# The low parts of the dense weights: a subtraction on VectorE, or an accumulating DMA

## The chip, the cores and the metric

The kernel runs on one core of a Trainium2 chip. A core has five engines with queues of their own: TensorE (PE in the profile, with PEld for its weight loads), VectorE (DVE), ScalarE (ACT), GpSimd (POOL) and SyncE (SP, which here only issues DMAs). DMAs run on 16 DMA engines of the core. The metric is the device time of one execution in microseconds, as the median of several runs.

## The reference

Two layers of a hybrid diffusion backbone over 512 latent tokens and 256 context tokens, width 1024, everything in float32. What it computes, cut to its products (the kernel's names of the weights):

```
a      = modulate(rms_norm(h))            # 1024 x 768 tokens
proj   = a @ w_in                         # 6656 columns: q, k, v, pool, Hyena inputs, gates
attn   = differential attention(q, k, v) @ w_attn_o
pool   = windowed means, mixed per group  @ w_pool_o
hyena  = two long convolutions, gated     @ w_hy_o
h      = h + g * ((sig0 * attn + sig1 * pool + sig2 * hyena) @ w_out)
h      = h + g * ((silu(gate) * up) @ w_ffn_out),  gate | up = modulate(rms_norm(h)) @ w_ffn_in
```

In layer 0 all 768 tokens go through; in layer 1 the context tokens give keys and values alone, so most of its products have 512 columns.

## The kernel before

Features lie on the 128 partitions, tokens along the free dimension. A float32 product is made of three products of shorter numbers: each operand is split into a high part, with the significand that one pass of TensorE carries, and a low part, the rest; TensorE then accumulates high*high, high*low and low*high in PSUM. The activations are split once. The weights are split as they come in.

The dense products go through `units` (L257). A unit is a list of steps; a step makes one tile of 128 output features (two tiles for the branch projections, which have only 4 input tiles): it loads up to 1024 weights per partition (512 KB) into `raw`, tag "wr" with 3 buffers, from SP's queue (L265); splits them by `split_to` (L250), a cast on ScalarE to `wh` (L252) and a subtraction on VectorE to `wl` (L253), tags "wh" and "wl" with 2 buffers each; and issues 8 x 3 matmuls for each range of token columns (L277), then its eviction. There are 328 steps. In layer 0 a step has two ranges, 512 and 256 columns, so 48 matmuls; in layer 1 one range of 512, so 24. Where a norm has to be finished for one range of tokens before the other (`cuts`: the output projection, the first units of the feed-forward, its last part), steps run over one range alone; those over 256 columns are the short steps.

The other work: the Hyena convolutions are done as block spectra, with transforms on TensorE and complex products on VectorE (`T`, `Y`, L801 to L822); their filters (`fa`, L695) likewise; attention has scores, exponentials and transposes. Modulation vectors are products and sums on VectorE from rows (`mr`) that SP loads beside everything else. Gate values and Hyena outputs go to DRAM and come back (`gsp`, `ysp`).

The order of the work: `PROG` and `HEAD` are orders written out by hand that mix convolution stages, attention and dense steps; within that a planner orders each engine's queue by priority and by when operands and buffers come free. From layer 0's first projections on, the weights' split has a priority 3000 instructions ahead (`ahead`, L957), so that it runs as soon as there is a buffer. Every queue is worked off in order. GpSimd has only 8 memsets: 4 constants and 4 that clear `qz` (L1201) before each layer's attention. Two other places borrow buffers of the tag "wr": three of the modulation weights' loads at the start (L382) and rows of `mod_steps` (L491).

Of the kernel before, what the change touches and what calls it, by code (L numbers as in the profile page):

```python
# [10 lines left out]
F32 = mybir.dt.float32  # L11
# [23 lines left out]
# columns of the vectors that hold one value per feature: first column, count of columns  # L35
# [6 lines left out]
# stages of the convolutions  # L42
# [67 lines left out]
def layouts(inp):  # L110
    """The inputs in the order in which the kernel reads them; every element is copied as it is."""
# [36 lines left out]
def build(ctx: ExitStack, tc: tile.TileContext, io: dict, out: bass.AP, dbg=None):  # L148
# [17 lines left out]
    def half(side, name, **tags):  # L166
        """Buffers on one side of the free memory, in this order, in place of those that the side had:
        tag = (bytes per partition, count)."""
        shut(side)
        st = ExitStack()  # L170
        pool = st.enter_context(tc.tile_pool(name=f"{name}_{side}", bufs=1, reuse_waits="tile", side=side))
        ph[side] = (st, tags)
        for t, (size, cnt) in tags.items():
            assert t not in tg, t
            tg[t] = (pool, size, cnt)
            pool.tile([P, size // 4], F32, tag=t, name=nm("first"), bufs=cnt)
# [25 lines left out]
    def FB(tag, n, dt=F32, shape=None):  # L202
        """Buffers of the background work: "fl" lives long, "fg" over two steps, "fx" shortly."""
        return PT(tag if tag in tg else "b", n, shape or [P, 512], dt)
# [22 lines left out]
    class Acc:  # L227
        """Output of a product for some ranges (first, count) of the 768 token columns."""
# [13 lines left out]
        def segs(self):  # L242
            """Per range."""
            return [(a, c, n) for a, (c, n) in zip(self.aps, self.rng)]

        def pieces(self):
            """As few contiguous pieces as there are."""
            return self.whole

    def split_to(hi, lo, src):  # L250
        """hi + lo = src, each with the significand that one pass carries."""
# [5 lines left out]
    def units(src, K, mts, xs, rng, evict):  # L257
        """A product cut into steps: a step loads and splits 1024 weights per partition or fewer, K of each
        output feature, multiplies and evicts. src(m): the weights of the step from output tile m on."""
        per = 2 if K <= 4 else 1  # L260

        def step(m):
            n = K * per * P
            raw = wp.tile([P, 1024], F32, tag="wr", name=nm("wr"), bufs=3)
            SP.dma_start(out=raw[:, 0:n], in_=src(m))  # L265
            wh = wp.tile([P, 1024], F32R, tag="wh", name=nm("wh"), bufs=2)
            wl = wp.tile([P, 1024], F32R, tag="wl", name=nm("wl"), bufs=2)
            with tc.high_priority(offset=ahead[0]):
                split_to(wh[:, 0:n], wl[:, 0:n], raw[:, 0:n])
# [29 lines left out]
    def spread(r, j0, n):  # L299
        """Columns of per-token values to a row, the same on every partition."""  # L300
# [6 lines left out]
    def sumsq_add(st, hk, c0, n):  # L307
        """st: per range, the sum over feature tiles of squares, one value per partition and token."""
# [15 lines left out]
    def norm_steps(hs, st, rng, g, sh, a):  # L324
        """Normalise and modulate one range of tokens into the split tiles of a, in steps."""
# [19 lines left out]
    def norm_more(n=1):  # L345
        """Emit n steps of the norm that goes on beside the products."""
# [13 lines left out]
    def first_norm(hs, mlp):  # L360
        """The first norm with the two vectors that it needs: the scale on TensorE, the shift on VectorE, as
        their weights arrive. The tokens come token-major and are scaled before they are transposed."""
# [15 lines left out]
        def load_shift():  # L378
            i = len(rows)
            src = io["w_mod"][0][i * P:(i + 1) * P, 0:1024]  # L380
            if i < 7:
                t = PT("y", "wm", [P, 1024]) if i < 4 else wp.tile([P, 1024], F32, tag="wr", name=nm("wr"), bufs=3)  # L382
# [91 lines left out]
    def mod_steps(todo):  # L474
        """Further vectors, one feature per partition, from the rows of the transposed weights: product and sum
        on VectorE, in steps. todo: (layer, vector, rows, streams)."""
# [7 lines left out]
        for l, n, i, nv in todo:  # L484
            pr = SM("pr", 32, bufs=1)
            pv = pr[:].rearrange("p (v h m) -> p v h m", v=2, h=2)
            for m in range(8):
                if "fx" in tg:
                    raw = [FB("fx", "mr")[:] for _ in range(2)]
                else:  # L490
                    t = wp.tile([P, 1024], F32, tag="wr", name=nm("mr"), bufs=3)  # L491
# [21 lines left out]
    def step():  # L513
        """One step of the work that waits in the background: what it weighs, or None."""
# [8 lines left out]
    def pump(n=1):  # L523
        """Emit steps that weigh n together."""
# [6 lines left out]
    def settle():  # L531
        """Go on to a point where the background work holds no buffer of the phase."""
# [3 lines left out]
    def finish(n=0):  # L536
        """Go on until n pieces of work are left."""
# [3 lines left out]
    def norm_cols(l, which, nv):  # L541
        """Columns gain*(1+scale) and shift for the norm before the mixers (0) or before the FFN (1)."""
# [41 lines left out]
    def sin_of(dst, src, b, f):  # L584
        """dst = sin(f * (src + b)), the argument brought into [-pi, pi] first."""
# [10 lines left out]
    def mlp_steps(l, res):  # L596
        """Hidden features of the filters, by lag and by descending lag in each block: the high parts on the half
        of the partitions of that number, the low parts on the other half."""
# [37 lines left out]
    def w3_cols(l, cg):  # L636
        """The last filter layer's weights of 128 channels, both directions and orders, on both halves of the
        partitions: high parts, low parts."""
# [6 lines left out]
    def filter_steps(l, mlp, cg, lat, rinv, seg_out):  # L645
        """Spectra of the kernel segments of 128 channels, both orders, segment 0 being the lowest lag:
        seg_out(segment) is called with a function that writes to a place [P, order, re/im, channel];
        and the inverse of the norm of order 0 and of the product of both norms, a column each."""
# [11 lines left out]
        def seg(dl, cur, cb, pr, pb):  # L660
            """K[dl] from the spectra of the lag blocks dl (cur, at cb) and dl - 1 (pr, at pb)."""
# [10 lines left out]
        for n, p in enumerate(pairs):  # L672
# [26 lines left out]
            if p == 0:  # L699
                # channel norms, a column per order, and the bias as a term of lag 0 on that scale  # L700
# [28 lines left out]
    def spectra(l, mlp, cg, lat):  # L729
        """The same into a tile [P, segment, order, re/im, channel]."""  # L730
# [9 lines left out]
    def spectra_steps():  # L740
        """The spectra of layer 1, in steps, to DRAM: re, im - re, re + im."""
# [19 lines left out]
    def load_spectra(cg):  # L761
        """The spectra of layer 1 of 128 channels, a tile [P, segment, part, channel] per order."""
# [8 lines left out]
    def forward(vh, vl, nb, parts):  # L771
        """Spectra of nb blocks of 128 tokens: [P, (-im, re, im) or (re + im, re, -im), block, channel]."""
# [18 lines left out]
    def spectral(K, oo, U, nb):  # L791
        """Products of the spectra, summed over the input blocks: [P, block, re/im, channel]."""
# [15 lines left out]
    def spectral_parts(K, U):  # L808
        """The same for four blocks with three real products each, from K = re, im - re, re + im."""
# [15 lines left out]
    class Conv:  # L825
        """Both long convolutions of 128 channels of one stream, in stages; the result replaces x2."""
# [67 lines left out]
    def hyena_in(l, a, cg):  # L894
        """The Hyena inputs of 128 channels after their short convolution, v, x1, x2: the units and their results."""
# [21 lines left out]
    swap = list(range(16, 32)) + list(range(0, 16))  # L917

    def layer(l, a, hs, first, prepare):
# [18 lines left out]
        # Hyena input with its short convolution, the long ones, and the gates between them  # L938
# [24 lines left out]
        def stage(what):  # L963
            """The next stage of a kind: gates (g), Hyena inputs (h), and of the convolutions, small letters for
# [573 lines left out]
```

## Time and profile before

| | before |
|---|---|
| time, three runs | 2394.32, 2396.85, 2397.19 us |
| median | 2396.85 us |
| the profiled execution | span 2393.1 us; its own time is not listed, 3.75 us beside the span lead to the median |
| granted TensorE clock, mean | 0.990 |
| busy: TensorE, VectorE, ScalarE, GpSimd | 97%, 73%, 41%, 0% |
| DMA | 302.47 MB, mean 126 GB/s |

A share of busy time is a mean over very different stages: the convolutions of layer 0 (about 60 to 720 us) load VectorE most, the feed-forward of layer 1 (about 2000 to 2393 us) almost only TensorE. The granted clock has two levels, 1.2 and 2.4 GHz; 1.00 in a stretch means 2.4 GHz throughout. A step's name in the rows is `d<-ah,wh` (or `hh`, `gh`, `xs`): product into PSUM tile d from activations and weights.

### The profile page before, as it was taken

The numbers are of one execution on the slowest core, as the hardware profiler recorded it, in microseconds if no ns is written. First come the engines' busy times: TensorE is split into PE (matmuls) and PEld (weight loads), VectorE is DVE, ScalarE is ACT, GpSimd is POOL, SyncE is SP. The second block draws the span as 40 slices with busy tenths as digits, with TensorE's granted clock in tenths as the row PEclk, the third lists the DMA queues.
The fourth block names the chain that finished last, engine by engine and source line by source line (L and its number), as shares of the span: only waits on it lengthen the run. The fifth ranks groups of instructions, "written<-read, shape, count | busy, mean of one in ns | idle before, by whom it ended". The sixth has DMA issues, their size and how long they took to land. (4 is left out here: it accounts for less than half of the span.)

```text
span 2393.1 us, 33367 instructions
## 1 busy us (share of the span) xinstructions
PE 2328.9 (97%) x12830; PEld 1981.6 (83%) x12830; DVE 1737.3 (73%) x3174; ACT 982.2 (41%) x1678; POOL 2.7 (0%) x8
## 2 busy tenths in 40 slices
PE   7999899999989999999999999999999999999998
PEld 2888788888878888888888888888888789888888
DVE  7688878899888785666768736899888778333336
ACT  6434343457772452111133424433377635322223
POOL 0000000000000000000000000000000000000000
PEclk9999899999999999999999999999999999999999
DMA  7132122322137553444725435344311444332224
GB/s 256 65 104 79 50 91 86 115 90 81 36 118 268 181 169 117 130 145 154 235 92 179 153 106 169 121 169 161 119 57 46 168 149 156 115 97 95 92 95 151
DMA packets 117369, 302.47 MB, mean 126 GB/s; under 512 B 13397, under 2 KB 27349, under 8 KB 116186
## 3 DMA queue, kind: packets, MB, share of 16 engines
q1 hardware_dynamic: 117210, 300.34, 37.2%
q8 instruction: 101, 1.65, 0.3%
q14 instruction: 58, 0.48, 0.1%
HBM read 266.74 MB, written 33.55 MB: 125 GB/s over the span
## 5 line engine op out<-in xcount | busy, mean ns | idle before, releaser
L277 PE MATMUL d<-ah,wh 128*128 128x512 f32 (+1 forms) x2336 | 712.1, 354 | 7.7 <-ACT si L1381 2.8
L252 ACT CAST wh<-wr 128x1024 fp32r<-128x1024 f32 (+3 forms) x328 | 331.6, 1011 | 936.2 <-PE d L277 770.2
L277 PE MATMUL d<-al,wh 128*128 128x512 f32 (+1 forms) x2336 | 713.9, 354 | 0.6 <-DVE al L470 0.5
L277 PE MATMUL d<-ah,wl 128*128 128x512 f32 (+1 forms) x2336 | 711.9, 353 | 2.1 <-DVE wl L253 2.0
L253 DVE TENSOR_TENSOR wl<-wr,wh 128x1024 fp32r<-128x1024 f32 (+3 forms) x328 | 384.4, 1173 | 161.3 <-ACT wh L252 150.0
L277 PEld LDWEIGHTS d<-ah,wh 128*128 128x128 f32 x2336 | 390.7, 188 | 72.7 <-ACT wh L252 3.4
L277 PEld LDWEIGHTS d<-ah,wl 128*128 128x128 f32 x2336 | 391.8, 189 | 63.8 <-DVE wl L253 3.0
L277 PEld LDWEIGHTS d<-al,wh 128*128 128x128 f32 x2336 | 392.1, 189 | 62.3 <-DVE al L340 0.8
L498 DVE SCALAR_TENSOR_TENSOR junk<-mr,cb 128x512 bf16<-128x512 f32 x256 | 176.2, 688 | 11.8 <-DMA mr<-in_w_mod_rows_dram 6.5
L277 PE MATMUL d<-hh,wh 128*128 128x512 f32 (+1 forms) x584 | 178.3, 339 | 3.7 <-DVE h L1416 3.7
L277 PE MATMUL d<-hh,wl 128*128 128x512 f32 (+1 forms) x584 | 177.6, 339 | 0.0
L277 PE MATMUL d<-hl,wh 128*128 128x512 f32 (+1 forms) x584 | 177.4, 339 | 0.0
L1390 DVE TENSOR_TENSOR si<-d,si 128x512 f32<-128x512 f32 (+2 forms) x48 | 36.9, 768 | 175.5 <-PE d L277 175.5
L277 PE MATMUL d<-xs,wh 128*128 128x512 f32 x576 | 144.6, 358 | 0.8 <-ACT mx L1193 0.5
L1416 DVE SCALAR_TENSOR_TENSOR h<-d,mod,h 128x512 f32<-128x512 f32 (+1 forms) x96 | 58.3, 614 | 81.3 <-PE d L277 79.7
L277 PEld LDWEIGHTS d<-hh,wh 128*128 128x128 f32 x584 | 102.0, 189 | 17.6 <-issue 4.0
L277 PEld LDWEIGHTS d<-hh,wl 128*128 128x128 f32 x584 | 101.8, 189 | 12.8
L277 PEld LDWEIGHTS d<-hl,wh 128*128 128x128 f32 x584 | 101.8, 189 | 12.8 <-DVE hl L253 0.2
L277 PEld LDWEIGHTS d<-xs,wh 128*128 128x128 f32 x576 | 94.7, 189 | 17.5 <-ACT mx L1193 0.9
L277 PE MATMUL d<-xs,wl 128*128 128x512 f32 (+1 forms) x288 | 87.3, 356 | 0.0
L805 DVE TENSOR_TENSOR Y<-Y,T 128x1024 f32<-128x1024 f32 (+1 forms) x80 | 84.5, 1056 | 0.2
L804 DVE TENSOR_TENSOR T<-U,K 128x1024 f32<-128x1024 f32 (+1 forms) x80 | 83.2, 1057 | 0.0
(296 smaller groups left out, 3211.4 us busy)
## 6 DMA issues: line engine op xcount, KB each, us to landing
wr<-in_w_in_dram SPq DMA_DIRECT2D x104, 512.0 KB, 3.3
wr<-in_w_ffn_in_dram SPq DMA_DIRECT2D x96, 512.0 KB, 3.4
mr<-in_w_mod_rows_dram SPq DMA_DIRECT2D x160, 256.0 KB, 3.3
wr<-in_w_out_dram SPq DMA_DIRECT2D x32, 512.0 KB, 4.2
ksp<-K SPq DMA_DIRECT2D x28, 384.0 KB, 3.0
K<-ksp SPq DMA_DIRECT2D x8, 1344.0 KB, 7.4
wr<-in_w_ffn_out_dram SPq DMA_DIRECT2D x24, 448.0 KB, 3.2
gsp<-gt SPq DMA_DIRECT2D x24, 384.0 KB, 2.4
```

What stands on the lines that cost most here:

```text
L252: A.copy(hi, src)
L253: V.tensor_tensor(out=lo, in0=src, in1=hi.bitcast(F32), op=ALU.subtract)
L277: PE.matmul(o, w[:, c0:c0 + P], x[k][xi][:, c:c + nn], start=(k == 0 and pi == 0), stop=(k == K - 1 and pi == 2))
L498: V.scalar_tensor_tensor(out=junk[:], in0=raw[hf], scalar=1.0, in1=cb[v][hf][:, 0:512], op0=ALU.mult, op1=ALU.mult, accum_out=pv[:, v, hf, ...
L804: V.tensor_tensor(out=t[:], in0=ub, in1=kb, op=ALU.mult)
L805: V.tensor_tensor(out=y[:], in0=y[:], in1=t[:], op=ALU.add)
L1390: V.tensor_tensor(out=sg[f][:, cs], in0=o, in1=sg[f][:, cs], op=ALU.mult)
L1416: V.scalar_tensor_tensor(out=hs[d][:, cs], in0=o, scalar=mods[l][:, 40 + d, s:s + 1], in1=hs[d][:, cs], op0=ALU.mult, op1=ALU.add)
```

## The change

A step no longer has a `raw` tile. The weights are loaded by GpSimd's queue straight into `wh`; ScalarE writes `wl` as -1 times `wh`; a second DMA of the same weights, also from GpSimd's queue, is added onto `wl` in place, which leaves weights minus high part. VectorE's subtraction is gone from these steps (other users of `split_to` keep it). The three tags "wr", "wh" and "wl" with 3 + 2 + 2 buffers become one tag "w" with 7. Both DMAs now lie in the priority block. Comments and docstrings are taken out as well.

```diff
         def step(m):
             n = K * per * P
-            raw = wp.tile([P, 1024], F32, tag="wr", name=nm("wr"), bufs=3)
-            SP.dma_start(out=raw[:, 0:n], in_=src(m))
-            wh = wp.tile([P, 1024], F32R, tag="wh", name=nm("wh"), bufs=2)
-            wl = wp.tile([P, 1024], F32R, tag="wl", name=nm("wl"), bufs=2)
+            wh = wp.tile([P, 1024], F32R, tag="w", name=nm("wh"), bufs=7)
+            wl = wp.tile([P, 1024], F32R, tag="w", name=nm("wl"), bufs=7)
             with tc.high_priority(offset=ahead[0]):
-                split_to(wh[:, 0:n], wl[:, 0:n], raw[:, 0:n])
+                G.dma_start(out=wh[:, 0:n], in_=src(m))
+                A.activation(wl[:, 0:n], wh[:, 0:n].bitcast(F32), AF.Copy, scale=-1.0)
+                G.dma_start(out=wl[:, 0:n], in_=src(m), accum_op=ALU.add)
             x = xs() if callable(xs) else xs
...
-                t = PT("y", "wm", [P, 1024]) if i < 4 else wp.tile([P, 1024], F32, tag="wr", name=nm("wr"), bufs=3)
+                t = PT("y", "wm", [P, 1024]) if i < 4 else wp.tile([P, 1024], F32, tag="w", name=nm("wr"), bufs=7)
...
-                    t = wp.tile([P, 1024], F32, tag="wr", name=nm("mr"), bufs=3)
+                    t = wp.tile([P, 1024], F32, tag="w", name=nm("mr"), bufs=7)
```

## Rows read from the trace of the kernel before

**Rows 1.** The page, part 1: busy us, share of span, instructions.

```profile
PE 2328.9 (97%) x12830; PEld 1981.6 (83%) x12830; DVE 1737.3 (73%) x3174; ACT 982.2 (41%) x1678; POOL 2.7 (0%) x8
```

**Rows 2.** Stretches, busy time of each engine; the first line names the columns.

```profile
core 0: us, PE busy (x) PEld busy (x) DVE busy (x) ACT busy (x) POOL busy (x), PEclk, DMA share, GB/s
240.00:300.00 60.00, 49.48 (x260) 42.24 (x259) 52.19 (x76) 20.75 (x36) 0.00 (x0) 0.86 0.14 45
...
480.00:540.00 60.00, 57.53 (x345) 49.52 (x344) 58.06 (x147) 33.01 (x74) 0.00 (x0) 1.00 0.26 89
...
660.00:720.00 60.00, 53.64 (x306) 44.95 (x305) 49.55 (x112) 43.04 (x94) 0.00 (x0) 0.91 0.36 128
720.00:780.00 60.00, 60.00 (x355) 52.95 (x354) 52.31 (x104) 14.02 (x16) 0.00 (x0) 1.00 0.78 265
...
1140.00:1200.00 60.00, 60.00 (x348) 52.99 (x347) 44.14 (x109) 10.86 (x12) 0.00 (x0) 1.00 0.71 237
...
1965.00:2033.00 68.00, 63.67 (x507) 61.14 (x505) 53.24 (x100) 37.56 (x62) 0.00 (x0) 1.00 0.46 156
2040.00:2340.00 300.00, 300.00 (x1315) 246.25 (x1314) 104.17 (x111) 78.24 (x95) 0.00 (x0) 1.00 0.30 97
...
2340.00:2384.00 44.00, 42.64 (x359) 41.85 (x357) 32.89 (x56) 21.57 (x34) 0.00 (x0) 1.00 0.53 162
```

**Rows 3.** Waits: engine, line, waited for: us in total, times, longest us.

```profile
POOL qz L1201 <- DVE T L820: 1242.5, 1, 1242.5
ACT wh L252 <- PE d L277: 770.2, 218, 7.3
...
PE yo L890 <- DVE Y L805: 5.4, 2, 5.1
...
PE fc L704 <- DVE fa L701: 4.1, 1, 4.1
...
PEld d L277 <- DVE wl L253: 4.0, 5, 1.1
...
PE d L277 <- DVE wl L253: 2.7, 4, 0.9
```

**Rows 4.** Chain of waits, 1955 to 2040 us: start us, us, what.

```profile
1965.04 1.06 ACT wh L252
...
1966.12 1.24 DVE wl L253
...
1967.40 19.94 PE d L277 x164
```

**Rows 5.** Groups of instructions by line: busy us, mean ns | idle before.

```profile
L253 DVE TENSOR_TENSOR wl<-wr,wh 128x1024 fp32r<-128x1024 f32 (+3 forms) x328 | 384.4, 1173 | 161.3 <-ACT wh L252 150.0 <-PE d L277 3.7 <-ACT sre L719 3.0
L252 ACT CAST wh<-wr 128x1024 fp32r<-128x1024 f32 (+3 forms) x328 | 331.6, 1011 | 936.2 <-PE d L277 770.2 <-issue 115.0 <-DMA mr<-in_w_mod_rows_dram 25.6
```

**Rows 6.** The scaled copies of line 414: min/median/max ns.

```profile
L414 ACT ACTIVATE xt<-xt,nz x3: 1135/1136/1148, 27.1 to 29.2; 128x1024 f32<-128x1024 f32 x3
```

**Rows 7.** DMA: queue, issues (KB, us to landing), SP's issues of line 265 (ns).

```profile
q1 hardware_dynamic: 117210, 300.34, 37.2%
...
wr<-in_w_in_dram SPq DMA_DIRECT2D x104, 512.0 KB, 3.3
wr<-in_w_ffn_in_dram SPq DMA_DIRECT2D x96, 512.0 KB, 3.4
...
xt<-in_x_dram SPq DMA_DIRECT2D x4, 512.0 KB, 8.2
...
w<-in_hf_w_dram SPq DMA_DIRECT2D x4, 16.0 KB, 1.9
...
L265 SPq DMA_DIRECT2D wr<-in_w_in_dram x104: 327/328/1157, 39.7 to 1827.2; - x104
```

## The prediction

> **What bounds the kernel now.** I read the busy line first. TensorE is busy for 2328.9 of 2393.1 us, VectorE for 1737.3, ScalarE for 982.2 and GpSimd for 2.7 [rows 1]. The span is 3.75 us short of the median run of 2396.85 us; I make the sum on the span and add those 3.75 us at the end, so changes can be set against 2396.85 directly. TensorE's idle time is therefore 64.2 us in all, and nothing that relieves another engine can give back more than that, plus what a lowered clock costs beside it.
>
> Second, the stretches [rows 2]: where is TensorE not full? From 240 to 300 us it is busy for 49.48 us at a granted clock of 0.86, with VectorE at 52.19 of 60; from 660 to 720 for 53.64 at 0.91; from 480 to 540 for 57.53 with VectorE at 58.06. These are the convolutions and the attention of layer 0, the only places where VectorE is nearly full while TensorE waits. From 2040 to 2340, the feed-forward of layer 1, TensorE is full for all 300 us and VectorE has only 104.17 us of work.
>
> Third, the waits [rows 3]: the longest of TensorE are 5.4 us for Y (spectral product) and 4.1 us for fa, both VectorE work of the convolutions. The wait for low weights (wl) is 2.7 us on the matmuls and 4.0 on the weight loads. ScalarE's 770.2 us in front of the high part (wh) is a wait for TensorE to let go of a buffer: the split runs ahead of the products and has slack. So the operation that the change removes is big on VectorE and nearly absent from what sets the end.
>
> Fourth, the chain of waits where it does show [rows 4]: between 1965 and 2033 us a cast of 1.06 us and a subtraction of 1.24 us stand in the chain in front of 164 matmuls, and this repeats. There a step has 24 matmuls on only 256 columns: 19.94 us / 164 = 122 ns each, 2.9 us a step. By the same working a step of layer 1's feed-forward takes 300 us / 1315 x 24 = 5.5 us, and one of layer 0 (two matmuls per weight tile, 48) 60 us / 348 x 48 = 8.3 us [rows 2].
>
> **The change part by part.**
>
> *VectorE's subtraction goes.* 328 of 1173 ns, 384.4 us of its 1737.3 [rows 5]. It gives time only where TensorE waits for VectorE. In 240 to 300 us the idle time is 10.5 us, and the matmuls after it run slowly; in 660 to 720 it is 6.4, in 480 to 540 2.5. VectorE is freed by a fifth, and the wait goes to the next item of its queue, so I take about two thirds: 8 + 4 + 1 = 13 us. Bounds: 0 (other VectorE work is just as late) and 35 us (all this idle time and the time lost at the lower clock beside it).
>
> *ScalarE's cast becomes a copy scaled by -1.* The cast of 128x1024 takes 1011 ns on the mean of its shapes [rows 5]; the nearest scaled copy is xt<-xt, 1136 ns [rows 6]. At most 328 x 0.13 = 43 us on an engine that is idle for 59% of the span: nothing.
>
> *The loads move from SP's queue to GpSimd's, and there are two.* SP spends 0.33 us on issuing one [rows 7]. The trace shows no DMA issued from GpSimd, so the bounds of one issue are 0.33 us and 1.9 us, the whole time from issue to landing of a load with hardly any data (16 KB, [rows 7]); I take 1 us. Two per step are 2 us against 2.9, 5.5 or 8.3: hidden, with little cover in the short steps. What else stands on GpSimd's queue are the clearings of qz, which waited 1242.5 us for VectorE's T [rows 3]; formerly nothing was queued behind them, now weight loads are. With two or three steps of weights in hand, the few us by which they may be late cost nothing. SP's other transfers no longer queue behind weight loads: a gain that nobody waits for.
>
> *The buffers.* Formerly 3 raw, 2 high and 2 low; a cast waited for the end of the step two before. In the ring of seven, in this order, step u's high part takes the buffer that step u-4 leaves, and its low part that of step u-3. After the negation, the accumulating DMA thus has two steps of TensorE to land: 5.8, 11 or 16.6 us. Load, copy, load in a row, with the trace's 3.3 us for 512 KB [rows 7], are about 1 + 3.3 + 1.1 + 1 + (3.3 to 5) = 10 to 11.5 us: covered in the long steps, not in the short ones, where three steps are 8.7 us.
>
> *The second transfer is the price.* All DMA moves 300.34 MB in 37.2% of 2393.1 us: 2.96 us per MB with 16 engines, 1.55 us per 512 KB step. The steps are 264 of 512 KB, 24 of 448, 24 of 384 and 16 of 320, 164 MB (the largest groups: [rows 7]). A second plain copy adds 164 x 2.96 = 486 us of DMA time; an accumulating one has to fetch the old content of its destination as well, two operands for one result. No row shows one. Bounds: one copy (1.55 us per step) and, from the first loads that land in 8.2 us with many in flight [rows 7], 6.2 us. I take two copies, 3.1 us, because it fetches twice the bytes. The share of DMA over the span goes from 38% to some 78%.
>
> The Trainium skill, "Collectives: The Full Stack", The bandwidth ceiling, says that an adding DMA is slow not for the addition but since it needs two source reads on one ring, and gives 31 GB/s against 62 for a copy. By it the price would be the same two copies; by the transfers of this trace alone, which are all copies, it would be one, and the change would be faster (first rival).
>
> Where does that not fit? (a) 1965 to 2033 us: the share is 0.46 of 68 us, 31 us, at 156 GB/s, 10.6 MB or 20 steps [rows 2]. With 20 x 3.1 it is 93 us: 25 us longer. (b) 2340 to 2384, the last short steps (448 KB): 0.53 x 44 = 23 us; 13 steps, after three in hand, add 13 x 2.7 = 35, so 58 against 44: 15 us (rounded up). (c) 720 to 780 at a share of 0.78 and 1140 to 1200 at 0.71: 7.2 steps each add 22 us, so 69 and 65 us in 60; half of the excess can move to neighbours with a lower share: 7 us. (d) The long steps of layer 1: 0.30 x 300 us + 55 x 3.1 = 260 of 300: fits, without much room. Sum: 25 + 15 + 7 - 13 = **+34 us: 2431 us, forecast 2430**.
>
> **The rivals.**
>
> 1. *The accumulation costs about one copy and VectorE's relief is what is left.* For it: addition need not slow a stream, and the largest part of the kernel has DMA shares under 0.5. Against it: a second fetch. With 1.55 us, (a) is 31 + 31 = 62 of 68 us, (b) 23 + 18 = 41 of 44, (c) fits but for 3%. Then the waits of the short steps for the split go too, 4.3 us in (a) and 1.4 in (b) [rows 2], minus the 13 us: about 2378 to 2385, say 2380, faster. It decides at 1.85 us per 512 KB, where (a) begins to exceed its 68 us.
>
> 2. *The accumulated part lands too late even for long steps.* From 9.5 us after its issue (two steps of 5.5 less the copy and the issue) layer 1's long steps (52 + 12 + 40 + 16 = 120 of projections, branches and feed-forward) are bound by the ring. At 12 us: (5.5 + 13.5) / 3 = 6.3 instead of 5.5 us per step, 100 us, and the short steps on top: 2550. For it: the loads of the start land in 8.2 us when many run. Against: only two or three would run here.
>
> 3. *GpSimd's order.* If the next high part is issued only behind the accumulation of the step before, which waits for the negation, a step cannot be shorter than 0.33 to 1 + 3.3 + 1.06 + 0.33 to 1, some 5 to 6.4 us. Steps of 5.5 just pass; the 33 short ones of (a) and (b) lose 2.2 to 3.5 us each, 73 to 115 us: about 2470.
>
> 4. *Nothing that can be measured:* loss in the short steps (an accumulation of about 2.3 us: (a) 10 us, (b) 3) equals the gain of 13: 2397.
>
> **How the numbers follow.** Forecast 0.40; rival 1 0.30; rival 2 0.10; rival 3 0.10; rival 4 0.10. 0.2% (4.8 us) is about what a measurement of this kernel can tell from no change. Faster has rival 1 and little else, 0.31; same is rival 4 and the edges of its neighbours, 0.12; slower is the rest, 0.57. The forecast's own range is 2405 to 2480. The range that is to hold 8 in 10 goes from 2378, rival 1's lower end, to 2530, short of the worst of rival 2; one that prices the accumulation at 6.2 us (DMA-bound throughout layer 1) is left out.
>
> **What would show it.** Right: VectorE's busy time near 1350 us; DMA share near 0.7 or more, with TensorE idle in the stretches of the short steps, waiting for a DMA into wl or for ScalarE's copy; the convolutions of layer 0 with less idle time. Wrong: transfers into wl that occupy the engines no longer than those into wh (rival 1), waits for wl spread over the feed-forward of layer 1 (rival 2), or waits of ScalarE for wh while the DMA engines are idle (rival 3).

## The result and the profile after

The changed kernel takes 2552.72 us (median of 4 runs, 2545.86 to 2559.65) against 2397.02 us for the kernel before beside it: a ratio of 1.0636 [1.0618, 1.0654], 152 us slower. The forecast was 34 us slower, 2430 us, with a range that ended at 2530. The direction was right and the size was not.

The page of the changed kernel, part 1 (busy us, share, instructions) and part 3 (queue: packets, MB, share of 16 engines; q0 is GpSimd's queue, q1 SP's):

```profile
PE 2373.8 (93%) x12830; PEld 2013.4 (79%) x12830; DVE 1390.8 (55%) x2846; ACT 983.9 (39%) x1678; POOL 468.5 (18%) x664
...
q0 software_dynamic: 94464, 328.25, 59.3%
q1 hardware_dynamic: 69978, 136.22, 15.5%
```

VectorE has lost 346.5 us of work [rows 1], and TensorE's idle time has grown from 64.2 to 168.7 us (2542.5 - 2373.8). The rest of the 149 us by which the span has grown goes with the lower clock beside idle time: TensorE is busy 44.9 us longer with the same instructions, at a mean granted clock of 0.975 instead of 0.990. The two queues now have some 75% of the DMA engines' time, where SP's had 37.2% [rows 7].

Stretches of the changed kernel. The first three lie at clock times of [rows 2], where by now slightly earlier work runs; 2053 to 2149.4 us has layer 1's first short steps, 2234 to 2354 the long steps of its feed-forward, 2467.8 to 2542.5 the last short ones:

```profile
core 0: us, PE busy (x) PEld busy (x) DVE busy (x) ACT busy (x) POOL busy (x), PEclk, DMA share, GB/s
240.00:300.00 60.00, 53.31 (x302) 45.87 (x302) 49.60 (x76) 23.44 (x40) 5.67 (x8) 0.97 0.46 106
480.00:540.00 60.00, 53.70 (x311) 46.23 (x310) 44.25 (x108) 28.67 (x60) 7.86 (x11) 0.97 0.62 159
...
720.00:780.00 60.00, 55.05 (x332) 48.49 (x331) 42.52 (x103) 21.23 (x37) 7.97 (x11) 0.94 0.90 269
2053.00:2149.40 96.40, 73.03 (x497) 70.01 (x496) 30.06 (x78) 36.79 (x60) 28.00 (x40) 0.88 0.97 223
2234.00:2354.00 120.00, 120.00 (x526) 98.26 (x525) 15.71 (x22) 30.20 (x36) 31.15 (x44) 1.00 0.91 190
2467.80:2542.50 74.70, 50.74 (x355) 47.07 (x353) 21.00 (x50) 20.50 (x32) 17.96 (x25) 0.88 0.84 191
```

Set against [rows 2]: the short steps now stand at a DMA share of 0.97 and 0.84, with TensorE busy for 73 of 96 and 51 of 75 us. The long steps of layer 1's feed-forward (2234 to 2354) lose nothing at a share of 0.91. From 240 to 300 us TensorE gains 4 us, from 480 to 540 it loses as much, but not at the same work: the first score of the attention falls at 506 us before and at 519 after. Over the whole stage up to that score, which holds the convolutions, TensorE's idle time has grown from 12.9 to 21.7 us: freeing VectorE made none of these stretches full.

Waits of the changed kernel (us in total, times, longest), the answer to [rows 3]:

```profile
POOL wh L267 <- PE d L277: 1339.3, 263, 21.2
ACT wl L268 <- PE d L277: 549.5, 148, 8.1
POOL wl L269 <- ACT wl L268: 449.8, 249, 15.0
...
DVE junk L498 <- DMA mr<-in_w_mod_rows_dram: 30.2, 29, 2.4
...
PE d L277 <- DMA wl<-in_w_ffn_out_dram: 25.0, 19, 2.4
...
PE d L277 <- DMA wl<-in_w_out_dram: 23.2, 15, 4.8
...
DVE g L686 <- DMA dec<-in_dec_dram: 21.6, 9, 5.0
```

TensorE now waits for the accumulation itself (`wl`), where it formerly waited 2.7 us for VectorE's low part. VectorE waits for loads of other work on SP's queue: `dec`, the decays of the filters, had 1.4 us in the kernel before, and `mr` 6.5.

The chain in the short steps, 2050 to 2080 us (start, us, what), in the place of [rows 4]:

```profile
2056.28 0.85 POOL wl L269
2057.13 0.56 POOL wh L267
2057.69 2.49 issue
...
2060.19 7.54 DMA wl<-in_w_out_dram
...
2067.77 4.31 PE d L277 x22
```

Instead of a cast of 1.06 and a subtraction of 1.24 us the chain goes through GpSimd's issues (0.85 and 0.56), 2.49 us in which GpSimd stands in front of the next accumulation (experiment 7 shows for what), and that accumulation, which lands after 7.54 us. ScalarE's part was forecast well, 1020 ns (formerly 1011 [rows 5]):

```profile
L268 ACT ACTIVATE wl<-wh 128x1024 fp32r<-128x1024 f32 (+3 forms) x328 | 334.7, 1020 | 1002.1 <-PE d L277 549.5 <-DMA wh<-in_w_ffn_in_dram 128.6 <-DMA wh<-in_w_ffn_out_dram 97.3
```

DMA issues (KB, median us to landing), set against [rows 7]: a load that landed 3.3 us after its issue takes 4.2, and the accumulation 7.2. The first rows are the changed kernel's, the second the kernel before's.

```profile
wh<-in_w_in_dram POOLq DMA_DIRECT2D x104, 512.0 KB, 4.2
wl<-in_w_in_dram POOLq DMA_DIRECT2D x104, 512.0 KB, 7.2
...
mr<-in_w_mod_rows_dram SPq DMA_DIRECT2D x160, 256.0 KB, 5.4
...
gsp<-gt SPq DMA_DIRECT2D x24, 384.0 KB, 5.9
...
dec<-in_dec_dram SPq DMA_DIRECT2D x40, 128.0 KB, 4.9
```

```profile
mr<-in_w_mod_rows_dram SPq DMA_DIRECT2D x160, 256.0 KB, 3.3
...
dec<-in_dec_dram SPq DMA_DIRECT2D x40, 128.0 KB, 2.9
```

Where the time went by stage, in us. The stages are cut at the same instructions of every kernel, so no shift of the clock blurs them: first dense product, first score of each layer's attention, and the first or last evictions of the output projection (L1350) and of the feed-forward (L1416). `no second` and `long only` are two of the experiments below: the second DMA left out everywhere, or in the short steps alone.

| stage | before | after | no second | long only |
|---|---|---|---|---|
| layer 0: first projections, convolutions | 453.8 | 465.2 | 447.9 | 465.6 |
| layer 0: attention, branches, to the output projection's eviction | 350.4 | 362.7 | 354.1 | 365.2 |
| layer 0: short steps, start of the feed-forward | 133.9 | 151.9 | 132.2 | 135.9 |
| layer 0: feed-forward, long steps | 267.9 | 268.4 | 266.6 | 270.9 |
| layer 0: feed-forward beside layer 1's spectra | 171.0 | 188.0 | 176.1 | 198.0 |
| layer 0: last part of the feed-forward (short) | 54.2 | 63.2 | 51.7 | 54.5 |
| layer 1: projections, convolutions, attention, merge | 481.6 | 499.4 | 480.8 | 501.9 |
| layer 1: output projection, start of the feed-forward (short) | 144.7 | 181.3 | 140.7 | 146.7 |
| layer 1: feed-forward, long steps | 233.8 | 233.5 | 233.5 | 233.5 |
| layer 1: last short steps, end | 49.4 | 74.7 | 50.8 | 49.6 |

After less before, the four short stages lose 18.0 + 9.0 + 36.6 + 25.3 = 88.9 us. The long steps of the two feed-forwards lose 0.5 and -0.3. The other four stages, long steps beside convolutions, attention and spectra, lose 11.4 + 12.3 + 17.0 + 17.8 = 58.5.

### The profile page after: what moved, and what is told of

It reads as the page before. It is cut to its first block, busy times and chain, and to the rows that moved or that the text cites. A ratio compares the mean times of both kernels' runs of the same rounds, so it can differ in the third digit from the quotient of the medians.

```text
span 2542.5 us, 33681 instructions
## 1 busy us (share of the span) xinstructions
PE 2373.8 (93%) x12830; PEld 2013.4 (79%) x12830; DVE 1390.8 (55%) x2846; ACT 983.9 (39%) x1678; POOL 468.5 (18%) x664
## 4 chain that ended last, share of the span: by engine, by line
PE 68%; DMA 11%; issue 9%; DVE 6%; ACT 4%; POOL 2%; SPq 0%; POOLq 0%; DVEq 0%; ACTq 0%
PE d L277 57%; DMA dec<-in_dec_dram 2%; DMA wl<-in_w_out_dram 2%; DMA wh<-in_w_in_dram 2%; POOL wl L269 1%; PE s L1063 1%; PE av L1119 1%; POOL wh L267 1%; DMA wl<-in_w_ffn_in_dram 1%; DMA wl<-in_w_ffn_out_dram 1%; DMA wl<-in_w_in_dram 1%; DMA w<-in_hf_w_dram 1%; PE sc L1064 1%; DVE Y L805 1%; PE at L1104 1%
## 5 line engine op out<-in xcount | busy, mean ns | idle before, releaser
L277 PE MATMUL d<-ah,wh 128*128 128x512 f32 (+1 forms) x2336 | 719.7, 357 | 5.8 <-ACT ah L467 2.4
L268 ACT ACTIVATE wl<-wh 128x1024 fp32r<-128x1024 f32 (+3 forms) x328 | 334.7, 1020 | 1002.1 <-PE d L277 549.5
L277 PEld LDWEIGHTS d<-ah,wh 128*128 128x128 f32 x2336 | 396.8, 191 | 69.4 <-ACT ah L467 2.5
L277 PEld LDWEIGHTS d<-al,wh 128*128 128x128 f32 x2336 | 398.2, 191 | 61.4 <-DVE al L470 0.2
L267 POOL DMA_DIRECT2D wh<-in_w_in_dram x104 | 59.5, 572 | 651.2 <-PE d L277 574.2
L1416 DVE SCALAR_TENSOR_TENSOR h<-d,mod,h 128x512 f32<-128x512 f32 (+1 forms) x96 | 57.4, 615 | 140.1 <-PE d L277 140.0
L269 POOL DMA_DIRECT2D wl<-in_w_in_dram x104 | 90.9, 874 | 217.3 <-ACT wl L268 148.7
L267 POOL DMA_DIRECT2D wh<-in_w_ffn_in_dram x96 | 56.2, 586 | 356.5 <-PE d L277 348.4
L277 PE MATMUL d<-gh,wl 128*128 128x256 f32 (+1 forms) x256 | 85.0, 332 | 23.3 <-DMA wl<-in_w_out_dram 23.2
```

What stands on the lines that cost most here:

```text
L267: G.dma_start(out=wh[:, 0:n], in_=src(m))
L268: A.activation(wl[:, 0:n], wh[:, 0:n].bitcast(F32), AF.Copy, scale=-1.0)
L269: G.dma_start(out=wl[:, 0:n], in_=src(m), accum_op=ALU.add)
L277: PE.matmul(o, w[:, c0:c0 + P], x[k][xi][:, c:c + nn], start=(k == 0 and pi == 0), stop=(k == K - 1 and pi == 2))
L1416: V.scalar_tensor_tensor(out=hs[d][:, cs], in0=o, scalar=mods[l][:, 40 + d, s:s + 1], in1=hs[d][:, cs], op0=ALU.mult, op1=ALU.add)
```

## The experiments

Differences between runs are taken from their ratios, as shares of 2397 us; the intervals make each good to some 4 to 8 us.

**1. The second transfer, taken apart: none, narrow, plain.** Three kernels change only the last line of the split. The order of TensorE's work nearly stays: with the plain transfer it is that of the changed kernel, and with the others some 220 of the trace's 12830 matmuls at most stand elsewhere (of the kernel before, some 2300). So what they show is hardly another order of work.

```diff
-                G.dma_start(out=wl[:, 0:n], in_=src(m), accum_op=ALU.add)
+                G.dma_start(out=wl[:, 0:n], in_=src(m))                                     # e1
+                (no second DMA)                                                             # e2
+                G.dma_start(out=wl[:, 0:64], in_=src(m)[:, 0:64], accum_op=ALU.add)          # e3
```

> The second transfer of the weights stays, with the same queue, wait and ring, but it overwrites wl instead of adding to it (the low part is then a second copy of the weights). Theory T1, engine time: a packet of 4 KB takes 327 ns when it accumulates and 159 when it loads; a short step needs 128 x (159 + 327) / 16 = 3.9 us of the DMA engines against 2.5 with two loads. Under T1 the time falls to about 2430 us, and the stretches of the short steps lose at most 10 us of the 60 that they lost. Theory T2, order and latency: load, copy, second transfer in a row, with seven buffers; a plain second transfer lands some 3 us sooner, so about 2480. Theory T3, GpSimd's queue and the planner's new order: unchanged, 2540 to 2555.

> The second transfer is left out, so wl holds the negated high part; VectorE is relieved as in the change. T1 and T2 both: the short steps are as fast as before or faster and the time is 2380 to 2400 us; by the prediction's gain for VectorE's relief it would be 2384. T3: 2430 or more, since the loads still come from GpSimd's queue in the new order.

> The accumulating transfer covers 64 of up to 1024 columns of wl; the rest of wl stays the negated high part. The waits, the order on GpSimd's queue and the fixed part of its landing stay, the bytes go. T1: 2385 to 2410 us. T2, if it is the row of load, copy and second landing and not its bytes: 2480 or more, with TensorE waiting for wl in the short steps.

Measured: no second transfer 2392.68 us, 0.9973 [0.9958, 0.9987]; narrow 2415.31, 1.0069 [1.0052, 1.0086]; plain 2461.90, 1.0263 [1.0234, 1.0292]. This makes four steps: everything but the second transfer (VectorE's relief, the move to GpSimd's queue, the ring) gives 6 us; a second transfer with hardly any data costs 23 us, its bytes as a copy 47, and what the accumulation takes beyond a copy 89. Narrow lies 5 us above the range of T1, engine time; plain lies between T1's 2430 us and T2's 2480. So neither theory has it alone. GpSimd's queue in the plain kernel and in the one without:

```profile
q0 software_dynamic: 94464, 328.25, 43.0%
...
wl<-in_w_in_dram POOLq DMA_DIRECT2D x104, 512.0 KB, 5.2
```

```profile
q0 software_dynamic: 47232, 164.12, 23.2%
...
wh<-in_w_in_dram POOLq DMA_DIRECT2D x104, 512.0 KB, 3.8
```

By these and the q0 of the changed kernel, 164.1 MB take 554 us as first loads (0.232 x 2387.4), 507 as a second copy (0.430 x 2467.7 - 554) and 954 accumulating (0.593 x 2542.5 - 554): 1.62 us per 512 KB as a copy, 3.05 accumulating, taking it that the first loads cost as much beside a second transfer as alone. The forecast had 1.55 and 3.1. So the price of the transfer was right, and it is not why the sum failed: already the plain copy, which the first rival had as the faster case, is 63 us slower than before.

The Trainium skill, "Collectives: The Full Stack", The bandwidth ceiling, lays the slowness of a collective's adding DMA on its two source reads. The trace agrees in size: 3.05 against 1.62 us, 1.9 times.

**2. GpSimd's queue alone.** The kernel before, with the raw weights loaded from GpSimd's queue.

```diff
-            SP.dma_start(out=raw[:, 0:n], in_=src(m))
+            G.dma_start(out=raw[:, 0:n], in_=src(m))
```

> The kernel before with one edit: the load of raw is issued by GpSimd and not by SP; split, buffers and VectorE's subtraction as before. T1, T2: 2397 us within 10. T3: slower by 30 us or more.

Measured 2402.74 us, 1.0014 [1.0005, 1.0024], 3 us. The move of queues is nearly free, as forecast.

**3. Short and long steps apart, first try.** One half of the steps keeps the accumulation, the other takes load, cast and subtraction as before, all in the ring of seven.

```diff
+                if sum(c for _, c in rng) <= 256:      # e5; e6 has > 256
+                    raw = wp.tile([P, 1024], F32, tag="w", name=nm("wr"), bufs=7)
+                    SP.dma_start(out=raw[:, 0:n], in_=src(m))
+                    split_to(wh[:, 0:n], wl[:, 0:n], raw[:, 0:n])
+                else: (as in the changed kernel)
```

> The change in all steps but the short ones (256 columns, 60 of 328), which load raw from SP's queue into the ring of seven and split on ScalarE and VectorE as the kernel before. In the traces the stretches of the short steps are 83 us longer with the change than before (12 + 9 + 37 + 25). Theory T1a, the DMA engines' time is what binds in the short steps and only there the whole price shows: 2553 - 83 = about 2470 us. Theory T4, the planner's order and late small loads everywhere are the larger part: above 2500.

> The mirror: only the 60 short steps accumulate, all others load raw from SP's queue and subtract on VectorE, in the ring of seven. T1a: 2398 + 83 = about 2480 us. T4: under 2440, since the rest of the kernel is undisturbed and the short steps alone would be planned around.

Measured: subtraction in the short steps 2538.29 us, 1.0579 [1.0556, 1.0601]; accumulation in the short steps alone 2499.30, 1.0403 [1.0375, 1.0432]. A subtracting step takes three buffers of the ring and an accumulating one two, so these measured the ring as well; the control in the next group says how much.

**4. The control for that, and the separation by omission.** The kernel before with its own split, but raw, high and low in one ring of seven (e11); and the changed kernel with the second DMA in long steps alone (e9) or in short steps alone (e10), again in the order of the changed kernel but for some 230 matmuls at most.

```diff
+                raw = wp.tile([P, 1024], F32, tag="w", name=nm("wr"), bufs=7)               # e11, wh and wl likewise
-                G.dma_start(out=wl[:, 0:n], in_=src(m), accum_op=ALU.add)
+                if sum(c for _, c in rng) > 256:                                            # e9; e10 has <= 256
+                    G.dma_start(out=wl[:, 0:n], in_=src(m), accum_op=ALU.add)
```

> The kernel before (load by SP, cast, VectorE's subtraction) with one ring of seven buffers for raw, high and low parts instead of 3 + 2 + 2; the control for the two mixed kernels. If the shared ring is harmless, as I took it to be: 2397 within 10. If it starves the short steps (three buffers a step, so two steps and a third in hand), 2420 or more, and the two mixed kernels have measured the ring as well.

> The change, but the 60 short steps leave the second transfer out (their wl stays the negated high part); two buffers of the ring per step in all steps, so nothing else is different. With the change at 2553 and no second transfer anywhere at 2393: T1a, the price is in the short steps' stretches (83 us by the traces): 2470 us. T4/T5, the price is mostly in the long steps that run beside other transfers: above 2500.

> The mirror: only the 60 short steps accumulate, the 268 long ones leave the second transfer out. T1a: 2393 + 83 = 2476 us. T4/T5: under 2440. If both parts simply add, this run and e9_short_none together are 2 x 2393 plus 160 us.

Measured: one ring 2470.59 us, 1.0295 [1.0275, 1.0315]: three tiles of a step in one ring of seven, with the load in the priority block too, cost 71 us without any second transfer, so the third group can't be read as a price of accumulation. Long only 2473.01, 1.0312 [1.0293, 1.0331]; short only 2480.46, 1.0342 [1.0327, 1.0358]. Against no second transfer that is 81 us for the long steps and 88 for the short ones; together 169, where both at once cost 159.

Where the long ones lose it: three stages of the kernel without a second transfer (layer 0's first one, layer 1's projections to merge, layer 1's long feed-forward), then the same stages with it in the long steps.

```profile
core 0: us, PE busy (x) PEld busy (x) DVE busy (x) ACT busy (x) POOL busy (x), PEclk, DMA share, GB/s
53.00:501.00 448.00, 436.83 (x2500) 378.55 (x2500) 334.26 (x522) 180.64 (x293) 21.60 (x40) 0.98 0.27 85
...
1481.50:1962.40 480.90, 476.40 (x2401) 396.08 (x2401) 341.22 (x646) 240.00 (x440) 35.49 (x67) 1.00 0.39 126
...
2103.10:2336.60 233.50, 233.49 (x1031) 191.66 (x1030) 31.37 (x44) 59.84 (x72) 23.31 (x44) 1.00 0.32 95
```

```profile
53.80:519.40 465.60, 442.32 (x2499) 382.91 (x2499) 334.26 (x522) 180.47 (x292) 56.97 (x80) 0.97 0.51 128
...
1543.80:2045.70 501.90, 480.81 (x2401) 397.79 (x2401) 340.50 (x646) 239.94 (x441) 93.04 (x132) 0.99 0.76 188
...
2192.40:2425.90 233.50, 233.49 (x1031) 191.63 (x1031) 31.38 (x44) 60.06 (x72) 59.80 (x85) 1.00 0.87 186
```

The losses do not follow the share: 17.7 us at 0.51, 21.0 at 0.76, none at 0.87. Nor is it other transfers as such: layer 0's long feed-forward has 91 loads of `mr` beside its weights, which land 6.1 us after their issue, at a share of 0.84 in the changed kernel, and loses 0.5 us; nothing on TensorE's path waits for them. The chain of waits says which transfers do stand in the way. In layer 0's feed-forward beside layer 1's spectra, first without, then with the accumulation in long steps (shares of the stage; the view cuts the line off):

```profile
by line: PE d L276 56.1%; DMA dec<-in_dec_dram 11.5%; DVE K L663 6.0%; issue 3.6%; DMA ksp<-K 2.6%; DVE K L748 2.4%; PE gre L710 1.9%; DVE g L685 1.6%; PE fg L681 1.5%; ACT sre L718 1.4%; PE gre L711 1.3%; PE gre L716 1.2%; PE fc L703 1.2%;
```

```profile
by line: PE d L278 45.4%; DMA ksp<-K 13.4%; DMA dec<-in_dec_dram 12.3%; DVE K L665 5.5%; issue 3.7%; DVE K L750 2.7%; DVE g L687 2.1%; PE gre L712 1.5%; DVE K L751 1.4%; PE gre L713 1.2%; ACT gh L252 1.0%; PE fg L683 1.0%; PE gre L718 1.0%;
```

`ksp` is a store of spectra from SP's queue whose buffer is wanted again; it goes from 2.6% of 176 to 13.4% of 198 us, 22 us more, as much as this stage loses; the store's landing goes from 3.1 to 4.8 us. But which transfer stands in the chain is not fixed. The changed kernel, with the same accumulations there, has `dec` in its place, from 1302 to 1480 us (shares of 178 us):

```profile
by line: PE d L277 43.6%; DMA dec<-in_dec_dram 16.3%; DVE K L664 6.8%; DMA ksp<-K 4.1%; issue 4.0%; DVE g L686 3.0%; DVE K L749 2.9%; PE gre L711 1.9%; DVE K L750 1.7%; ACT sre L719 1.7%; PE gre L717 1.3%; PE fc L704 1.2%; PE gre L712 1.2%;
```

In layer 1's projections to merge of the kernel with the accumulation in long steps it is the weights themselves:

```profile
by line: PE d L278 50.9%; issue 6.4%; DMA wh<-in_w_in_dram 4.2%; PE av L1120 3.2%; PE dx L278 2.8%; PE s L1064 2.8%; DVE T L821 1.9%; DMA wh<-in_w_attn_o_dram 1.7%; PE at L1105 1.7%; PE sc L1065 1.4%; DMA wh<-in_w_hy_o_dram 1.4%; DMA wl<-in
```

There 4.2% of 502 us, 21 us, are loads of `wh` into TensorE's way, which without the accumulation don't appear among the lines that the view shows of that stage (down to 0.9%). These are readings of chains, and the next pair shows how far they carry.

**5. Without the decay loads.** One suspect taken away: `dec` (40 loads of 128 KB) is no longer loaded, and the filters are multiplied by a resident tile instead; in the changed kernel (e7), and in the kernel before as its control (e8).

```diff
-            dc = FB("fx", "dec", shape=[P, 2, P])
-            SP.dma_start(out=dc[:], in_=io["dec"][q0 + (p + nb) // 2, cg])
-                            in1=dc[:].rearrange("p b (o c) -> p b o c", o=1).to_broadcast([P, 2, 2, P]),
+                            in1=cols[0][:, 0:P].rearrange("p (b o c) -> p b o c", b=1, o=1).to_broadcast([P, 2, 2, P]),
```

> The change, with the loads of the filters' decays (dec, 40 of 128 KB) left out: the product takes 128 columns of a constant instead. With the change these loads land in 4.9 us and not in 2.9, and in the chain of waits from 1302 to 1480 us they are 16%, 29 us. Theory T5, small loads that are issued just in time land late because the accumulations fill the DMA engines: 2510 to 2530 us, the gain in the stretches of the filters (54 to 519 and 1302 to 1478). Rival: the chain only passes over to ksp or to VectorE: 2545 to 2553.

> Control for the run before: the kernel before with the decays' loads left out in the same way. There they stand in no wait over 1.4 us: 2397 us, at most 4 less.

Measured: 2544.18 us, 1.0593 [1.0559, 1.0627], and 2411.36, 1.0047 [1.0031, 1.0063]. The changed kernel gains 10 us, where T5 had 23 to 43 and the rival 0 to 8. The control loses 11, although it does less; without these loads the planner puts some 2000 of TensorE's 12830 matmuls elsewhere, which is the likely reason and not shown. So an edit that lets the planner reorder can't be read to better than about 11 us, and the late `dec` loads are worth some 20 us of the 81 at most.

**6. Six buffers instead of seven.**

```diff
-            wh = wp.tile([P, 1024], F32R, tag="w", name=nm("wh"), bufs=7)
+            wh = wp.tile([P, 1024], F32R, tag="w", name=nm("wh"), bufs=6)      # and the others of this tag
```

> The change with six buffers in the ring instead of seven. T1 (the DMA engines' time binds): a little slower, at most 40 us, in the short steps. T2 (the row of load, copy and second transfer binds, so that what is in hand decides): 100 us or more slower, since half a step of 5.5 us less in hand exposes the accumulation's 7.4 us in the long steps of layer 1.

Measured 2909.53 us, 1.2132 [1.2111, 1.2152]. A stretch of 22 long steps of layer 1, which take 120 us with seven buffers (2234 to 2354, above), and the waits from 2517 to 2806 us:

```profile
2517.00:2663.00 146.00, 129.66 (x527) 102.38 (x526) 15.69 (x22) 30.45 (x37) 31.35 (x44) 0.95 0.70 158
```

```profile
POOL wl L269 <- ACT wl L268: 151.9, 39, 7.4
...
ACT wl L268 <- DMA wh<-in_w_ffn_in_dram: 128.7, 26, 7.7
```

A step takes 6.64 us instead of 5.45 while the DMA engines do less (0.70 against 0.91). So here the row of load, copy and accumulation decides, as the ring's depth divides it: rival 2's ring, but not its condition, for accumulations landed 5.2 us after their issue, far below its 9.5. With six buffers three steps have to hold the row and the step itself; with this kernel's landings (6.1 for the load, 5.2 for the accumulation, 1.0 for the copy) that is (12.3 + 5.5) / 3 = 5.9 us. The rest, up to 6.64, is not taken apart. The first of the two waits, rival 3's order, is a candidate: in 289 us GpSimd stands for 151.9 in front of accumulations whose negation is not done, with the next load behind. With seven buffers the long steps fit, but one buffer from where they don't.

**7. The short steps: engine time or the row?** Instead of accumulating, a short step stores `wl` twice to DRAM, which nobody reads; the queue is GpSimd's (e13), ScalarE's (e15) or SP's (e16). The long steps have no second transfer.

```diff
-                G.dma_start(out=wl[:, 0:n], in_=src(m), accum_op=ALU.add)
+                if sum(c for _, c in rng) <= 256:
+                    for _ in range(2):
+                        G.dma_start(out=scr[nscr[0], :, 0:n], in_=wl[:, 0:n])     # e15: A, e16: SP, through a float32 view
+                        nscr[0] += 1
```

> Like e10_short_only, but in place of the accumulation each of the 60 short steps stores wl twice to a scratch area in DRAM (512 KB each, from GpSimd's queue, at the place of the accumulation). No matmul waits for the stores; long steps have no second transfer, wl stays the negated high part everywhere. The stores use about as much DMA engine time as one accumulation (two copies). T1, engine time: the short steps are as slow as in e10, about 2480 us. T2, the row: TensorE does not wait, 2393 to 2410 us; 2410 to 2430 if the stores hold GpSimd's queue up.

> As e13_store_twice, but ScalarE's queue issues the two stores of wl, right behind the copy that writes it, so that GpSimd's queue holds the loads of the high parts alone. T1, engine time: about 2480 us as in e10_short_only. T2, the row of load, copy and accumulation: 2393 to 2410 us.

> The same with SP's queue issuing the stores, which stand there among the loads of the residual and the gates. T1: about 2480 us. T2: 2395 to 2415 us. If this and e15_store_act differ by more than 15 us, a queue and not the DMA engines decides.

Measured: 2492.80 us, 1.0401 [1.0384, 1.0419]; 2463.34, 1.0254 [1.0236, 1.0272]; 2437.33, 1.0148 [1.0131, 1.0165]. Against no second transfer that is 103, 67 and 42 us for the same bytes, by the queue they stand on; the accumulation costs 88. ScalarE's and SP's queues differ by 25 us, more than the 15 that the expectation had set: a queue has a part, and not the DMA engines alone. From GpSimd's queue the stores hold up the weight loads queued behind them: from 1985 to 2110 us it stood for 85.0 us in front of stores whose negation was not done. From SP's queue they fill the engines; 1988 to 2060 us there, and in the kernel with accumulation in the short steps alone:

```profile
1988.00:2060.00 72.00, 58.70 (x408) 53.84 (x407) 26.20 (x70) 32.53 (x54) 8.98 (x17) 0.92 1.04 375
```

```profile
1988.00:2060.00 72.00, 54.81 (x374) 52.11 (x372) 18.43 (x47) 23.12 (x36) 20.47 (x29) 0.88 0.94 216
```

In engine time two stores are close to an accumulation: by the queues' shares those of all short steps took 143 us (22.3% of 2429.2, less the 16.1% of 2478.5 that SP's queue has without them), the accumulations 162 (28.9% of 2478.5, less the 554 of the first loads). But the stores also keep the buffer of `wl` until they have landed, and loads wait for it, here from 1988 to 2110 us of the run on SP's queue:

```profile
POOL wh L269 <- DMA scr<-wl: 27.4, 8, 4.6
```

So full engines explain about half of the 88 us at most. The other half goes with the row through GpSimd's queue, as the 61 us between the two queues suggest. The changed kernel's GpSimd there (start, us, what, idle before):

```profile
2056.25 0.88 POOL L269 DMA_DIRECT2D wl<-in_w_out_dram  x1 [2.45 <-ACT ssq L312]
2056.80 0.89 POOL L267 DMA_DIRECT2D wh<-in_w_out_dram  x1
2060.19 0.87 POOL L269 DMA_DIRECT2D wl<-in_w_out_dram  x1 [2.50 <-ACT wl L268]
...
2064.75 0.87 POOL L269 DMA_DIRECT2D wl<-in_w_out_dram  x1 [3.13 <-ACT wl L268]
...
2070.48 0.87 POOL L269 DMA_DIRECT2D wl<-in_w_out_dram  x1 [4.29 <-ACT wl L268]
```

An accumulation every 3.9 to 5.7 us, mean 4.7, where a step has 24 matmuls of 122 ns, 2.9 us [rows 4]. Each load stands right behind an accumulation that waits for a negation. A load and an accumulation of 512 KB are also 1.6 + 3.05 = 4.7 us of engine time: both limits lie at the same place, and the runs don't part them further.

**8. The subtraction on GpSimd.** Another way to relieve VectorE: the kernel before, with the same subtraction on GpSimd.

```diff
-                split_to(wh[:, 0:n], wl[:, 0:n], raw[:, 0:n])
+                A.copy(wh[:, 0:n], raw[:, 0:n])
+                G.tensor_tensor(out=wl[:, 0:n], in0=raw[:, 0:n], in1=wh[:, 0:n].bitcast(F32), op=ALU.subtract)
```

> The kernel before with the weights' subtraction on GpSimd in place of VectorE: no second transfer, three tags of buffers as before. If VectorE's relief is what e2_no_second showed, and GpSimd can do 128x1024 within a step: 2388 to 2395 us. If GpSimd needs over 2.9 us for one, the short steps wait: 2400 to 2460.

Measured 2601.54 us, 1.0845 [1.0822, 1.0868]: the worst of the kernels with the buffers of before. The expectation had it faster if GpSimd needed less than 2.9 us.

```profile
L270 POOL TENSOR_TENSOR wl<-wr,wh 128x1024 fp32r<-128x1024 f32 (+3 forms) x328 | 800.4, 2441 | 1773.3 <-ACT wh L269 1654.5 <-PE d L278 79.6 <-PE sp L304 14.7
...
L806 DVE TENSOR_TENSOR Y<-Y,T 128x1024 f32<-128x1024 f32 (+1 forms) x80 | 98.9, 1236 | 0.4
```

It takes 2441 ns, twice VectorE's 1173 [rows 5], and VectorE's own product `Y` of two tiles went from 1056 to 1236 ns. The Trainium skill, "SBUF — State Buffer", Who interferes with whom, says that a VectorE operation with two SBUF inputs contends with a GpSimd one that reads SBUF; the trace agrees, by 17% on `Y`. How the 204 us divide is not taken apart; 42 of them fall before layer 0's first score, where there are no short steps.

No kernel here that computes the low parts is faster than the one before. The one without a second transfer is 6 us faster, but it has none: in this order and with this ring, 6 us is the most that this way of relieving VectorE could have brought.

## Why the prediction was wrong

**What bounds the kernel, and the sign: right.** VectorE's subtraction was nearly absent from what sets the end, and the transfer in its place was not.

**Relief of VectorE, 13 us: too high.** The kernel without the second transfer has all of it and the rest of the edit, and gains 6. VectorE fell to 1390.8 us (1350 were forecast), and of TensorE's 64.2 us of idle time 63.2 stayed there (2387.4 - 2324.2).

**Copy, issues and queue: right.** 1020 ns for the copy; GpSimd issues a load in 0.54 us and an accumulation in 0.87 (1 us was taken); its queue costs 3 us.

**The price of the second transfer: right.** 3.05 us per 512 KB, 3.1 forecast. Rival 1 falls with it, and twice over: at one copy's price the kernel would not be faster but 63 us slower.

**The step that failed most: (c), 7 us for the second transfer in stretches where it shares the engines with other work, all else "fits".** I added the new engine time to the old, and where the sum stayed below the stretch I put down nothing. In the long steps of layer 1's feed-forward that holds, at 0.91 and without loss. So it does in layer 0's, the place of 1140 to 1200 us, to which (c) gave 2.5 of its 7. But where a transfer lands just before its use, time was lost at shares of 0.5 to 0.8: the long steps cost 81 us. A free share means that the work fits over the stretch; a load that is waited for pays the longer landing (`dec` 2.9 to 4.9 us, `mr` 3.3 to 5.4) or the longer row (loads of `wh` 3.3 to 4.2 and more) each time. By the chains it was `ksp` or `dec` in layer 0's last long steps and the weights in layer 1's projections. That these waits cost the 81 us is read from chains and not shown by a run, and how the 81 us divide is not settled, since taking `dec` away also changed the order of the work.

**(a) and (b), 40 us for the short steps: 88.** Their two stretches were priced at 25 and 15 us; the stages that hold them lost 36.6 and 25.3. Layer 0 also has short steps, and these the sum left out: 27 us. The row was priced at 10 to 11.5 us; with 5.4 to 6.7 us for a load and 6.9 to 7.4 for an accumulation to land it is 14 to 16, and the sum let the engines' time alone set the pace. Two stores of the same size cost 42 us on another queue, so engine time is about half of it at most.

**(d), the long steps of layer 1's feed-forward fit: right**, but by one buffer.

**Rival 2** did not happen with seven buffers: accumulations landed 7.4 us after their issue, below its 9.5. With six the ring did bind the long steps, by its depth and not by a later landing. **Rival 3** had a part in the short steps: GpSimd waits for negations with the next load behind. Its price, 73 to 115 us for the short steps of (a) and (b), was somewhat nearer to the 62 us that their stages lost than the forecast's 40, but full engines hold them at the same pace. **Rival 4** is out. The sum as measured: -6 for the rest of the edit, +88 short, +81 long, less 11 that they share: +152.

## What to carry to other kernels

Before a transfer is doubled, ask of every stretch not only whether the DMA engines have room but which loads there are waited for, and price their longer landing; spare share is no slack for a load that is late by a microsecond. An accumulating DMA cost the engines about two copies here, and it adds its whole landing to the row from load to use, so count buffers against load + copy + accumulation at landing times under load, and test one buffer less: here a single buffer was worth 357 us (2909.53 against 2552.72). An engine's busy share is no reason to relieve it: 346 us of VectorE's work were worth 6.

## What the runs showed of the hardware

- An accumulating DMA of 512 KB landed 7.2 us after its issue, where a plain one in its place landed in 5.2; packets of 4096 bytes on GpSimd's queue fall into two groups there, around 174 and 328 ns; without the second transfer, loads alone, their median is 174.
- Loads of the weights from GpSimd's queue took 159 ns per packet of 4096 bytes into a float32 tile (the kernel of experiment 2), as from SP's queue, and 174 into a float32r tile.
- Six buffers instead of seven made the changed kernel 14% longer, with the DMA engines less busy.
- Two stores of 512 KB per short step cost 42 us on SP's queue, 67 on ScalarE's and 103 on GpSimd's.
- GpSimd's subtraction of 128x1024 took 2441 ns and made VectorE's two-input products 10 to 17% longer (`T` 1057 to 1165, `Y` 1056 to 1236).
